# A block of two mixers and routed experts on one core: low parts of projection pieces on VectorE, scores of two heads by turns in two banks, norms for 128 tokens

## The chip, the core and the metric

The kernel runs on one core of a Trainium2 chip. A core has TensorE (matmuls and weight loads, results in PSUM), VectorE, ScalarE, GpSimd, and SyncE, whose queue (SP) issues most transfers to 16 DMA engines. The metric is the device time of one execution in microseconds, median of several runs.

## What is computed

One layer over 2048 tokens of width 1024: a modulated norm, one projection `w_in` of 5792 columns, two recurrent mixers on parts of it, two output projections that are gated and summed, then a router and 32 experts of which each token takes two. The part that matters here is the second recurrence's set-up (RWKV-7, 8 heads of 64):

```
p = p + mu * (prev - p)
r, k, v, wd, ad, gd = split(p)
kk = heads(k * k_k)
kk = kk * rsqrt(maximum(sum(kk * kk, axis=-1), 1e-24))
# per token: state = state * w + (state @ -kk) (kk * a)^T + v k^T ;  y = state @ r
```

and the projection itself, `proj = h @ w_in`, in fp32 accuracy.

## The kernel before

**Projections.** `w_in` is applied in four rounds (g = 0..3) of 512 tokens and 46 tiles of 128 columns (`win_tiles`). fp32 accuracy comes from splitting both sides into a high part (rounded to fp32r) and a low part (the rest): each tile is 8 x 3 matmuls of 128x512 (lines 778 to 780). A tile's weights are two pieces of 512 x 128 (`parts`). In round 0 a piece is loaded raw (two raw buffers, line 759), ScalarE makes its high part (760), GpSimd its low part (761), and SP stores both for the later rounds (763), which load them ready-made (756). Pieces have four buffers. The evicted tile goes to DRAM (line 794). `mixed` does the same for the two output projections, with 16 pieces split once.

**Mixers.** The 2048 tokens go through both mixers in 16 blocks of 128. For the RWKV mixer, `rw_prep` sets a block up: norms of `kk` per head (matmuls with `hind`, line 196), then scores of each chunk of 64 tokens: for each half `hp` of the partitions (heads are stacked two to a tile, 64 rows each) four matmuls into the one bank `rp` (224) and four VectorE instructions that scale and mask them into `Gc` (226). From `Gc` a 32x32 triangular system is cut out through DRAM (`Nd`, `Nl`), solved by a recurrence of 62 VectorE instructions (243, 244) and brought back (`Pd`, `Pa`). `rw_chain` (matmuls `mm` of line 296, `px<-R,Pa` among them) runs the state over the chunks, and `hg_block` is the other mixer (HGRN2), whose transposes and outputs use the bank `ht` and whose score levels use `hl`. The five banks `rp`, `xy`, `px`, `ht`, `hl` and three of the projections fill PSUM.

**Order.** Instructions are recorded in the code's order, which lays projection tiles between the mixers' pieces (`fill`), and are then put in order per engine by the framework's scheduler. Each engine and SP's queue run in that order and wait where a semaphore is not yet there. From the experts on the order is the program's own.

Of the kernel before, what the change touches and what calls it, by code (L numbers as in the profile page):

```python
# [6 lines left out]
FP = mybir.dt.float32  # L7
# [3 lines left out]
AF = mybir.ActivationFunctionType  # L11
OP = mybir.AluOpType
# [5 lines left out]
TB = 128  # L18
# [130 lines left out]
def rw_prep(k, b):  # L149

    nc = k.nc
    NC = TB // 64
    g, off = divmod(b * TB, 512)
    wk, w2p, ps = k.wk, k.wk2, k.ps
# [15 lines left out]
    for i, (bias, dst) in enumerate(((k.w0, sw), (k.a0, a))):  # L170
        pt = ps.tile(f4, FP, name="rp")
# [14 lines left out]
    kkr = wk.tile(f4, FP, name="t3")  # L186
    nc.gpsimd.tensor_tensor(kkr, k_, k.kkc[:, :, None].to_broadcast(f4), OP.mult)
    AR = w2p.tile([128, 4, NC, 128], FP, name="AR", bufs=2); BK = wk.tile([128, 4, NC, 128], FP, name="BK")
    c4 = lambda t: t.rearrange("p m (c t) -> p m c t", t=64)
    sq = BK[:, :, :, 64:128]; nc.scalar.activation(sq, c4(kkr), AF.Square)  # L190

    pt = ps.tile(f4, FP, name="rp")
    nrm = pt[0:64, 0, 0:8 * NC].rearrange("p (c h) -> p c h", c=NC)
    for c in range(NC):
        for m in range(4):
            nc.tensor.matmul(nrm[:, c, 2 * m:2 * m + 2], sq[:, m, c], k.hind, start=(c + m == 0), stop=True,
                             skip_group_check=True)
    iv = k.iv[b % 2]
    nc.vector.tensor_scalar(iv[0:64], nrm, 1e-24, 2.0, op0=OP.max, op1=OP.mult)
    nc.vector.reciprocal(iv[0:64], iv[0:64])  # L200
    nc.gpsimd.tensor_tensor(AR[:, :, :, 64:128], c4(r_), c4(Gm), OP.mult)
    ARf = AR.rearrange("p m c x -> p (m c) x")
# [14 lines left out]
    Gs = []  # L217
    for c in range(NC):
        Gc = w2p.tile([128, 2, 4, 128], FP, name="Gc", bufs=4)
        for hp in range(2):  # L220
            pt = ps.tile([128, 4, 128], FP, name="rp")
            h = slice(hp * 64, hp * 64 + 64)
            for m in range(4):
                nc.tensor.matmul(pt[:, m], BK[h, m, c, :], AR[h, m, c, :], start=(m == 0), stop=True, skip_group_check=True)  # L224
            for m in range(4):
                nc.vector.scalar_tensor_tensor(Gc[:, hp, m], pt[:, m], iv[:, c, 2 * m + hp:2 * m + hp + 1], k.gmask, op0=OP.mult, op1=OP.mult)  # L226
        for hf in range(2):
            q = slice(hf * 32, hf * 32 + 32)
            nc.sync.dma_start(Nd[hf, c * 8:(c + 1) * 8].rearrange("x s t -> s x t"), Gc[q, :, :, q].rearrange("p a m t -> p (a m) t"))
        Gs.append(Gc)  # L230
# [24 lines left out]
    for c in range(NC):  # L255
        pt = ps.tile([128, 512], FP, name="rp")
        for m in range(4):
            nc.tensor.transpose(pt[:, m * 128:(m + 1) * 128], BK[:, m, c, :], k.ident)
        t = w2p.tile([128, 4, 128], FP, name="BT", bufs=4)
# [5 lines left out]
    for c2 in range(NC // 2):  # L265
        pt = ps.tile([128, 512], FP, name="rp")
# [10 lines left out]
    pt = ps.tile(f4, FP, name="rp")  # L277
# [473 lines left out]
def parts(k, key, src):  # L751

    nc = k.nc
    w = k.ld.tile([128, 2, 4, 128], FR, name="w", bufs=4)
    if key in k.split:
        nc.sync.dma_start(w.bitcast(FP), k.split[key])
        return w
    raw = k.ld.tile([128, 4, 128], FP, name="wraw", bufs=2)
    nc.sync.dma_start(raw, src.rearrange("(k p) n -> p k n", p=128))
    nc.scalar.copy(w[:, 0], raw)  # L760
    nc.gpsimd.tensor_tensor(w[:, 1], raw, w[:, 0].bitcast(FP), OP.subtract)  # L761
    k.split[key] = k.dr1.tile([128, 2, 4, 128], FP, name="W" + key)
    nc.sync.dma_start(k.split[key], w.bitcast(FP))
    return w


def win_tiles(k, I, hT, g, tiles):

    nc = k.nc
    dst_of = {"rw": k.RWP, "hg": k.HGP, "gt": k.GTP}  # L770
    hi, lo = hT
    for group, ti, c0 in tiles:
        dst = dst_of[group]
        W = [parts(k, f"{group}{ti}_{q}", I['w_in'][0, q * 512:(q + 1) * 512, c0:c0 + 128]) for q in range(2)]
        pt = k.pm.tile([128, 512], FP, name="mm", bufs=3)
        for kk in range(8):
            whi, wlo = (W[kk // 4][:, j, kk % 4] for j in range(2))
            nc.tensor.matmul(pt, whi, hi[kk // 2][:, kk % 2], start=(kk == 0), stop=False)  # L778
            nc.tensor.matmul(pt, whi, lo[kk // 2][:, kk % 2], start=False, stop=False)  # L779
            nc.tensor.matmul(pt, wlo, hi[kk // 2][:, kk % 2], start=False, stop=(kk == 7))  # L780
        ev = k.ld.tile([128, 512], FP, name="ev", bufs=3)
        if group == "rw":
            nc.scalar.activation(ev, pt, AF.Identity, scale=k.omu[:, ti:ti + 1])  # L783
            mu = k.mu[:, ti:ti + 1]; ca = k.carry[:, ti:ti + 1]
            nc.vector.scalar_tensor_tensor(ev[:, 1:512], pt[:, 0:511], mu, ev[:, 1:512], op0=OP.mult, op1=OP.add)  # L785
            nc.vector.scalar_tensor_tensor(ev[:, 0:1], ca, mu, ev[:, 0:1], op0=OP.mult, op1=OP.add)
            nc.vector.tensor_copy(ca, pt[:, 511:512])
        else:
            k.flip ^= 1
            if k.flip:  # L790
                nc.scalar.copy(ev, pt)
            else:
                nc.vector.tensor_copy(ev, pt)
        nc.sync.dma_start(dst[g][ti], ev)
# [620 lines left out]
def build(ctx, tc, I, out, NE=32):  # L1415
# [22 lines left out]
    with ExitStack() as c2:  # L1438
# [15 lines left out]
        for g in range(5):  # L1454
# [14 lines left out]
            for i in range(4 if g < 4 else 2):  # L1469
                b = g * 4 - 2 + i  # L1470
                ws = WS[i] if g < 4 else MS[i]
                if g == 4 and i == 1:
                    list_init(k)
                    router_consts(k, I)
                with hp(tc, b + 1 >= HP[0]):
                    nxt = rw_prep(k, b + 1) if -1 <= b < 15 else None
                fill(ws[0])
                if b >= 0:
                    with hp(tc, b >= HP[1]):
                        rw_chain(k, b, prep)  # L1480
                fill(ws[1])
                if b >= 0:
                    with hp(tc, b >= HP[2]):
                        hg_block(k, b)
                fill(ws[2])
                prep = nxt
# [37 lines left out]
```

## Time and profile before

| | |
|---|---|
| median of 3 runs | 2983.82 us (2966.77 to 2990.27) |
| profiled execution | 2984.66 us, span 2982.8 us |
| TensorE matmuls busy | 2766.5 us (93%) |
| weight loads | 2257.7 us (76%) |
| VectorE, ScalarE, GpSimd | 1985.8 us (67%), 1286.4 us (43%), 943.0 us (32%) |
| mean granted TensorE clock | 0.965 |

Busy times are sums over the whole span and say little about one stage: the span holds a start of some 45 us, the four rounds with the mixers (to about 1830 us), the output projection and the router (to about 2210 us) and the experts. In the rows below PE is TensorE's matmuls, PEld its weight loads, DVE VectorE, ACT ScalarE, POOL GpSimd, SPq SyncE's queue; PEclk is the granted clock as a share of full speed. A matmul's duration overlaps the next one's start, so prices are read from starts. An fp32 matmul stands as two passes, a projection matmul as one.

### The profile page before, as it was taken

How to read it: one execution, taken by the hardware profiler on the slowest of the kernel's cores; microseconds unless marked ns; L12 is line 12 of the kernel's file. 1: busy time of each engine (PE TensorE's matmuls, PEld its weight loads, DVE VectorE, ACT ScalarE, POOL GpSimd, SP SyncE). 2: the span in 40 equal slices, each digit the busy share in tenths (PEclk: the TensorE clock that was granted, in tenths of full speed). 3: DMA queues.
4: the chain of work that ended last, by engine and by line, in shares of the span. 5: the costliest groups of instructions: out<-in, count | busy, mean ns of one | idle time of the engine just before them, and what ended most of it. 6: DMA issues, size and time to landing. Idle time of an engine off the chain costs nothing. (4 is left out here: it accounts for less than half of the span.)

```text
span 2982.8 us, 45842 instructions
## 1 busy us (share of the span) xinstructions
PE 2766.5 (93%) x15562; PEld 2257.7 (76%) x15562; DVE 1985.8 (67%) x4010; ACT 1286.4 (43%) x2188; POOL 943.0 (32%) x1092
## 2 busy tenths in 40 slices
PE   6989999999999999999999999899959999999992
PEld 4667788887888888888888777788857777777771
DVE  6164666683677666677547876446565798989983
ACT  4332544432343523333233544322224566767772
POOL 3344643322332313342233453332441121112112
PEclk9989999999999999999999989999979999999996
DMA  8897786687565776566555678886448799999996
GB/s 257 285 322 239 224 256 196 196 252 219 174 211 176 232 246 191 180 223 202 187 183 173 187 231 289 302 294 212 142 158 256 264 363 347 363 347 359 373 314 229
DMA packets 460698, 734.65 MB, mean 246 GB/s; under 512 B 115569, under 2 KB 277361, under 8 KB 460354
## 3 DMA queue, kind: packets, MB, share of 16 engines
q1 hardware_dynamic: 448114, 696.68, 69.8%
q0 software_dynamic: 11088, 29.60, 4.3%
q10 hardware_dynamic: 1152, 4.19, 0.4%
q8 instruction: 165, 2.70, 0.4%
q14 instruction: 179, 1.47, 0.1%
HBM read 561.81 MB, written 175.39 MB: 247 GB/s over the span
## 5 line engine op out<-in xcount | busy, mean ns | idle before, releaser
L778 PE MATMUL mm<-hThi,w 128*128 128x512 f32 x1472 | 596.4, 406 | 19.1 <-ACT hThi L667 10.1
L780 PE MATMUL mm<-hThi,w 128*128 128x512 f32 x1472 | 595.4, 405 | 9.2 <-POOL w L761 8.6
L779 PE MATMUL mm<-hTlo,w 128*128 128x512 f32 x1472 | 592.1, 402 | 1.0 <-DVE hTlo L668 0.9
L1206 DVE TENSOR_TENSOR wlo<-raw,whi 128x1024 fp32r<-128x1024 f32 x404 | 484.1, 1254 | 46.1 <-ACT whi L1205 21.5
L1205 ACT CAST whi<-raw 128x1024 fp32r<-128x1024 f32 x408 | 405.7, 1057 | 206.0 <-PE U L931 48.6
L778 PEld LDWEIGHTS mm<-hThi,w 128*128 128x128 f32 x1472 | 282.3, 192 | 88.2 <-ACT hThi L667 10.2
L780 PEld LDWEIGHTS mm<-hThi,w 128*128 128x128 f32 x1472 | 282.0, 192 | 79.5 <-POOL w L761 20.2
L779 PEld LDWEIGHTS mm<-hTlo,w 128*128 128x128 f32 x1472 | 282.1, 192 | 61.2 <-DVE hTlo L668 3.6
L1294 POOL DMA_INDIRECT X<-y,lists x33 | 72.3, 2190 | 497.4 <-DVE y L1292 449.6
L243 DVE TENSOR_TENSOR pr<-Pl,Nl 128x2 f32<-128x2 f32 (+30 forms) x496 | 202.5, 408 | 12.0
L451 POOL TENSOR_TENSOR Xq<-h,kf 128x256 f32<-128x256 f32 x96 | 80.2, 835 | 399.0 <-PE hl L470 116.9
L761 POOL TENSOR_TENSOR w<-wraw,w 128x512 fp32r<-128x512 f32 x108 | 145.2, 1346 | 171.0 <-ACT w L760 153.4
L760 ACT CAST w<-wraw 128x512 fp32r<-128x512 f32 x108 | 66.8, 619 | 152.1 <-DMA wraw<-in_w_in_dram 114.0
L244 DVE TENSOR_REDUCE Pl<-pr 128x1 f32<-128x2 f32 (+30 forms) x496 | 124.0, 250 | 12.0
L856 PE MATMUL mm<-hThi,w 128*128 128x512 f32 x256 | 104.9, 412 | 11.7 <-ACT hThi L667 6.8
L296 PE MATMUL xy<-UV,Gc 128*64 128x64 f32 (+1 forms) x1536 | 114.0, 223 | 0.6 <-ACT UV L305 0.6
L1236 PE MATMUL G<-whi,xh 128*128 128x512 f32 x256 | 104.9, 410 | 9.5 <-PEq L1367 8.3
L296 PEld LDWEIGHTS xy<-UV,Gc 128*64 128x64 f32 (+1 forms) x1536 | 95.6, 127 | 19.4 <-issue 7.1
L857 PE MATMUL mm<-hTlo,w 128*128 128x512 f32 x256 | 105.3, 411 | 2.4 <-DVE hTlo L668 2.4
L785 DVE SCALAR_TENSOR_TENSOR ev<-mm,mu,ev 128x511 f32<-128x511 f32 x56 | 41.8, 747 | 97.1 <-ACT ev L783 93.5
L226 DVE SCALAR_TENSOR_TENSOR Gc<-rp,iv,gmask 128x128 f32<-128x128 f32 x256 | 71.9, 343 | 51.7 <-PE rp L224 51.4
L858 PE MATMUL mm<-hThi,w 128*128 128x512 f32 x256 | 103.8, 406 | 0.0
(492 smaller groups left out, 5924.3 us busy)
## 6 DMA issues: line engine op xcount, KB each, us to landing
raw<-in_exp_w_gate_dram SPq DMA_DIRECT2D x126, 512.0 KB
raw<-in_exp_w_up_dram SPq DMA_DIRECT2D x126, 512.0 KB
raw<-in_exp_w_down_dram SPq DMA_DIRECT2D x124, 512.0 KB
w<-Whg SPq DMA_DIRECT2D x96, 512.0 KB
w<-Wgt SPq DMA_DIRECT2D x96, 512.0 KB
w<-Wrw SPq DMA_DIRECT2D x84, 512.0 KB
wraw<-in_w_in_dram SPq DMA_DIRECT2D x92, 256.0 KB
Whg<-w SPq DMA_DIRECT2D x32, 512.0 KB
```

Source lines behind the costliest of these rows:

```text
L243: nc.vector.tensor_tensor(pv, Pl[:, :ni, :ns], Nl[:, :ns, t_][:, None, :].to_broadcast([128, ni, ns]), OP.mult)
L244: nc.vector.tensor_reduce(Pl[:, :ni, t_], pv, AX.X, OP.add)
L296: mm = lambda *a_, **kw: nc.tensor.matmul(*a_, skip_group_check=True, **kw)
L761: nc.gpsimd.tensor_tensor(w[:, 1], raw, w[:, 0].bitcast(FP), OP.subtract)
L778: nc.tensor.matmul(pt, whi, hi[kk // 2][:, kk % 2], start=(kk == 0), stop=False)
L779: nc.tensor.matmul(pt, whi, lo[kk // 2][:, kk % 2], start=False, stop=False)
L780: nc.tensor.matmul(pt, wlo, hi[kk // 2][:, kk % 2], start=False, stop=(kk == 7))
L856: nc.tensor.matmul(pt, w[:, 0, kk], hi[o // 2][:, o % 2], start=(kk == 0), stop=False)
L857: nc.tensor.matmul(pt, w[:, 0, kk], lo[o // 2][:, o % 2], start=False, stop=False)
L1205: s.nc.scalar.copy(hi, raw)
L1206: eng.tensor_tensor(lo, raw, hi.bitcast(FP), OP.subtract)
L1236: mm = lambda *a, **kw: nc.tensor.matmul(*a, skip_group_check=True, **kw)
```

## The change

1. `parts`: the low part of a piece (line 761) is computed by VectorE and not by GpSimd.
2. `rw_prep`, norms: four matmuls for 128 tokens (line 195 after) take the place of eight for 64 tokens (line 196 before); two VectorE instructions bring them to the 64 rows of `iv`. The squares lie in the first half of `BK`'s bytes instead of every second 64 columns.
3. `rw_prep`, scores: the eight matmuls of a chunk are written head by head in turn, one on partitions 0 to 63 into `rp`, one on 64 to 127 into `ht` (line 223 after); the evictions follow.

```diff
-    sq = BK[:, :, :, 64:128]; nc.scalar.activation(sq, c4(kkr), AF.Square)
+    sq = BK.rearrange("p m c x -> p (m c x)")[:, 0:4 * TB].rearrange("p (m t) -> p m t", t=TB); nc.scalar.activation(sq, kkr, AF.Square)
     pt = ps.tile(f4, FP, name="rp")
-    nrm = pt[0:64, 0, 0:8 * NC].rearrange("p (c h) -> p c h", c=NC)
+    nrm = pt[:, 0, 0:8]
+    for m in range(4):
+        nc.tensor.matmul(nrm[:, 2 * m:2 * m + 2], sq[:, m], k.hind, start=(m == 0), stop=True, skip_group_check=True)
+    iv = k.iv[b % 2]
     for c in range(NC):
-        for m in range(4):
-            nc.tensor.matmul(nrm[:, c, 2 * m:2 * m + 2], sq[:, m, c], k.hind, start=(c + m == 0), stop=True,
-                             skip_group_check=True)
-    iv = k.iv[b % 2]
-    nc.vector.tensor_scalar(iv[0:64], nrm, 1e-24, 2.0, op0=OP.max, op1=OP.mult)
+        nc.vector.tensor_scalar(iv[0:64, c], nrm[c * 64:c * 64 + 64], 1e-24, 2.0, op0=OP.max, op1=OP.mult)
...
-        for hp in range(2):
-            pt = ps.tile([128, 4, 128], FP, name="rp")
-            h = slice(hp * 64, hp * 64 + 64)
-            for m in range(4):
+
+        pts = [ps.tile([128, 4, 128], FP, name=n) for n in ("rp", "ht")]
+        for m in range(4):
+            for h, pt in zip((slice(0, 64), slice(64, 128)), pts):
                 nc.tensor.matmul(pt[:, m], BK[h, m, c, :], AR[h, m, c, :], start=(m == 0), stop=True, skip_group_check=True)
+        for hp, pt in enumerate(pts):
             for m in range(4):
                 nc.vector.scalar_tensor_tensor(Gc[:, hp, m], pt[:, m], iv[:, c, 2 * m + hp:2 * m + hp + 1], k.gmask, op0=OP.mult, op1=OP.mult)
...
-    nc.gpsimd.tensor_tensor(w[:, 1], raw, w[:, 0].bitcast(FP), OP.subtract)
+    nc.vector.tensor_tensor(w[:, 1], raw, w[:, 0].bitcast(FP), OP.subtract)
```

What the scheduler makes of it is seen in the order of the instructions. On VectorE, in round 0 during the first block's set-up (`acc` belongs to the modulation's sums, `ev` to evicted tiles), before:

```order
L213 TENSOR_TENSOR BK<-t_1177,t_1210 128x8x64
L657 TENSOR_SCALAR ev<-mm,A_424,mod_422 128x128
L635 TENSOR_TENSOR xss_1594<-xss_1594 128x1
L86 TENSOR_SCALAR rst_x<-xss_1594 128x1
L226 SCALAR_TENSOR_TENSOR Gc<-rp,iv_510,gmask 128x128 x4
L607 TENSOR_SCALAR acc<-xin,cs 128x512
```

and in the changed kernel:

```order
L761 TENSOR_TENSOR w<-wraw,w 128x512
L793 COPY ev<-mm 128x512
L226 SCALAR_TENSOR_TENSOR Gc<-rp,iv_510,gmask 128x128 x4
L226 SCALAR_TENSOR_TENSOR Gc<-ht,iv_510,gmask 128x128 x4
L657 TENSOR_SCALAR ev<-mm,A_424,mod_422 128x128 x2
L761 TENSOR_TENSOR w<-wraw,w 128x512
L609 SCALAR_TENSOR_TENSOR acc<-xin,cs,acc 128x512
```

The low parts of pieces now stand in VectorE's queue among evictions that wait for TensorE, and both halves of a chunk's scores are evicted one after the other.

On TensorE, in round 1, a chunk's scores before (`px` and `xy` are the RWKV chain's):

```order
L779 MATMUL mm<-hTlo_8108,w 128x512
L224 MATMUL rp<-AR,BK 128x128 x4
L296 MATMUL px<-UV,BT 128x128 x4
L296 MATMUL xy<-UV,Gc 64x64 x8
L780 MATMUL mm<-hThi_8102,w 128x512
...
L780 MATMUL mm<-hThi_8103,w 128x512
L224 MATMUL rp<-AR,BK 128x128 x4
L778 MATMUL mm<-hThi_8103,w 128x512
```

and a chunk's scores of a block in the changed kernel's round 1, where the turns go on to eight rows:

```order
L779 MATMUL mm<-hTlo_8087,w 128x512
L296 MATMUL px<-UV,BT 128x128 x2
L223 MATMUL rp<-AR,BK 128x128
L223 MATMUL ht<-AR,BK 128x128
L223 MATMUL rp<-AR,BK 128x128
L223 MATMUL ht<-AR,BK 128x128
...
L223 MATMUL ht<-AR,BK 128x128
L296 MATMUL px<-UV,BT 128x128 x2
```

Two runs of four with projection matmuls between them became one run of eight that changes halves at each matmul.

On TensorE in another block of that round of the changed kernel (`ht<-Shg,Xq` and `ht<-vT,scT` are the other mixer's outputs, `ht<-ident,o` its last transposes):

```order
L503 MATMUL ht<-Shg,Xq 128x128 x4
L505 MATMUL ht<-vT,scT 128x128 x4
L508 MATMUL hl<-vT,kT 128x128 x4
L223 MATMUL rp<-AR,BK 128x128 x4
L296 MATMUL px<-R,Pa 32x64 x8
...
L520 MATMUL ht<-ident,o_11119 128x128 x4
L296 MATMUL px<-UV,BT 128x128 x2
...
L778 MATMUL mm<-hThi_8082,w 128x512
L779 MATMUL mm<-hTlo_8086,w 128x512
L223 MATMUL ht<-AR,BK 128x128 x4
```

Here the half that goes to `rp` stands together and the half that goes to `ht` stands some 45 rows later, behind the other mixer's use of that bank.

## Rows read from the trace of the kernel before

**Rows 1.** Stretches: busy us (instructions) of each engine, PEclk, DMA share, GB/s.
```profile
core 0: us, PE busy (x) PEld busy (x) DVE busy (x) ACT busy (x) POOL busy (x), PEclk, DMA share, GB/s
...
60.00:160.00 100.00, 88.91 (x361) 64.23 (x359) 21.01 (x57) 31.54 (x58) 38.50 (x34) 0.99 0.88 280
160.00:260.00 100.00, 88.52 (x410) 67.06 (x409) 67.69 (x158) 35.14 (x82) 47.21 (x47) 0.87 0.88 283
260.00:400.00 140.00, 135.19 (x801) 108.21 (x801) 72.55 (x168) 58.89 (x110) 76.60 (x80) 0.96 0.78 241
400.00:1750.00 1350.00, 1329.87 (x8582) 1105.90 (x8581) 899.93 (x2206) 509.67 (x1025) 443.09 (x600) 0.99 0.66 205
```

**Rows 2.** Timeline, a score run: start us, us, engine line op out<-in xcount.
```profile
601.71 0.39 PE L778 MATMUL mm<-hThi,w 128*128 128x512 f32 x1
602.02 1.16 PE L224 MATMUL rp<-AR,BK 64*128 64x128 f32 x8
...
603.69 0.40 PE L778 MATMUL mm<-hThi,w 128*128 128x512 f32 x1
...
604.39 0.39 PE L778 MATMUL mm<-hThi,w 128*128 128x512 f32 x1
...
602.02 0.96 PEld L224 LDWEIGHTS rp<-AR,BK 64*128 64x128 f32 x8 [0.36 <-DVE h L425]
```

**Rows 3.** Timeline of TensorE, a run of eight passes on all 128 rows.
```profile
650.54 0.40 PE L780 MATMUL mm<-hThi,w 128*128 128x512 f32 x1
650.78 1.00 PE L479 MATMUL hl<-Xq 128*128 128x64 f32 x8
...
652.13 0.39 PE L780 MATMUL mm<-hThi,w 128*128 128x512 f32 x1
```

**Rows 4.** Timeline of TensorE, a run of the norms.
```profile
1616.42 0.40 PE L779 MATMUL mm<-hTlo,w 128*128 128x512 f32 x1
1616.95 1.09 PE L196 MATMUL rp<-hind,BK 128*64 128x2 f32 x16
...
1618.54 0.40 PE L779 MATMUL mm<-hTlo,w 128*128 128x512 f32 x1
```

**Rows 5.** Timeline of SP, ScalarE and GpSimd, one piece's way in round 0.
```profile
88.81 0.43 SPq L759 DMA_DIRECT2D wraw<-in_w_in_dram  x1
...
92.47 0.62 ACT L760 CAST w<-wraw 128x512 fp32r<-128x512 f32 x1 [0.70 <-DMA wraw<-in_w_in_dram]
...
93.17 1.29 POOL L761 TENSOR_TENSOR w<-wraw,w 128x512 fp32r<-128x512 f32 x1 [2.57 <-ACT w L760]
94.48 0.32 SPq L763 DMA_DIRECT2D Wrw<-w  x1
...
94.85 0.43 SPq L759 DMA_DIRECT2D wraw<-in_w_in_dram  x1
```

**Rows 6.** A stretch, instructions of line 778 alone: PE busy (x), PEld busy (x).
```profile
60.00:160.00 100.00, 46.37 (x116) 21.78 (x116) 0.99 0.88 280
```

**Rows 7.** A stretch of three tiles at a steady pace, columns as in rows 1.
```profile
97.00:115.00 18.00, 17.35 (x73) 12.86 (x72) 3.10 (x9) 5.79 (x9) 6.79 (x7) 1.00 0.94 301
```

**Rows 8.** Lines 761 and 668: count, ns min/median/max, first and last start us.
```profile
L761 POOL TENSOR_TENSOR w<-wraw,w x108: 1257/1287/2610, 42.0 to 1769.0; 128x512 fp32r<-128x512 f32 x108
...
L668 DVE TENSOR_TENSOR hTlo<-rwin,hThi x3: 715/1030/1136, 46.0 to 48.1; 128x512 fp32r<-128x512 f32 x3
```

**Rows 9.** Timeline of VectorE beside GpSimd, and line 213's durations.
```profile
174.11 1.29 POOL L761 TENSOR_TENSOR w<-wraw,w 128x512 fp32r<-128x512 f32 x1
174.18 1.76 DVE L213 TENSOR_TENSOR BK<-t,t 128x512 f32<-128x512 f32 x1 [1.37 <-POOL t L212]
...
L213 DVE TENSOR_TENSOR BK<-t,t x16: 665/809/3319, 174.2 to 1726.2; 128x512 f32<-128x512 f32 x16
```

**Rows 10.** Timeline, a block's last score evictions and the first matmul on `Pa`.
```profile
1568.31 1.13 DVE L226 SCALAR_TENSOR_TENSOR Gc<-rp,iv,gmask 128x128 f32<-128x128 f32 x4 [4.63 <-PE rp L224]
...
1623.19 0.52 PE L296 MATMUL px<-R,Pa 32*32 32x64 f32 x6
```

**Rows 11.** VectorE's waits from 160 to 420 us: total us, times, longest us.
```profile
DVE BT L260 <- PE rp L258: 13.7, 4, 8.6
DVE Gc L226 <- PE rp L224: 13.6, 5, 6.8
DVE scT L480 <- PE hl L479: 11.0, 4, 4.8
DVE ev L793 <- ACT w L760: 8.9, 1, 8.9
```

## Prediction

> **What bounds the kernel now.** I read the stretches first, then the TensorE timeline inside them, then the queues. Between 400 and 1750 us, 45% of the span, TensorE is busy for 1329.9 of 1350 us at a granted clock of 0.99, while VectorE, ScalarE and GpSimd stand at 67%, 38% and 33% [rows 1]. There the time is the sum of what TensorE has to do, and only less TensorE work (or a new hole in it) moves the end. Before 400 us it is less full: 88.9 us of 100 between 60 and 160, 88.5 of 100 at a clock of 0.87 between 160 and 260, 135.2 of 140 after that [rows 1]. From 1800 us on nothing is touched except the last two blocks of the mixers. The part from the experts on stands in the same order in both programs.
>
> What TensorE does with the touched matmuls is seen when a run of them stands alone between projection matmuls. Three projection matmuls take 0.70 us (603.69 to 604.39) [rows 2]. A run of 8 score passes (4 matmuls of fp32, two passes each, 64 rows by 128 columns) makes 1.98 us of what would be 0.70, so it costs 1.28 [rows 2]. A run of 8 passes that uses all 128 rows costs 1.59 - 0.70 = 0.89 us, 0.112 a pass [rows 3]. The passes themselves are alike, so entering and leaving the half array costs 1.28 - 0.89 = 0.39 us a run. The norms' run (16 passes, 128 rows by 64 columns, 0.06 us each) costs 2.12 - 0.70 = 1.42 us, of which 16 x 0.06 = 0.96 is passes and 0.46 is entering and leaving [rows 4].
>
> In the first round (60 to 160 us) something else is the limit: a loop. A piece's load is issued at 88.81, its cast starts at 92.47 when it has landed, GpSimd's low part runs from 93.17 to 94.46, SP stores the piece at 94.48 and issues the load that reuses the raw buffer at 94.85 [rows 5]. That is 6.04 us for one of two raw buffers, so one tile (two pieces) in 6.04 us, where TensorE needs 24 x 0.233 = 5.6. Over the whole stretch 116 matmuls of line 778, eight to a tile, make 14.5 tiles in 100 us, 6.9 us each [rows 6].
>
> **The low parts (line 761): 108 pieces, 92 of them in the first round.** GpSimd takes 1.29 us at the median; VectorE's nearest row, the same subtraction on 128x512, took 0.715 at its shortest and about 1.03 beside a busy GpSimd [rows 8]. I take 0.7, so the loop loses 0.6 and becomes 5.44, under TensorE's 5.6. SP's order helps too: both loads of a tile now stand ahead of the store of an evicted tile. But the DMA engines were 94% busy in a stretch at that pace of 6.04 [rows 7], which puts their own floor at about 5.7 us. Bounds: 0 if the transfers only take longer, 14.5 x (6.9 - 5.6) = 19 us if TensorE is always fed. Nearest to the rows is the loop's 0.6 cut by the DMA floor: 14.5 x 0.5 = **-7 us**. From 160 to 400 us the tiles are slowed by the mixers, not by this loop: 0. The 16 pieces of the output projections, near 1750 us: 0.
>
> VectorE gets 108 x 0.7 = 76 us more. It is busy 21% to 68% of these stretches [rows 1]; its idle time is the cover, and it is thin where VectorE waits for others with pieces queued behind (the slower rival). Something comes back: its subtraction of line 213 took 1.76 us beside GpSimd's line 761 against 0.665 at its shortest [rows 9], so each piece taken from GpSimd also takes such a block away. Both stay at 0 in the sum, since VectorE is not the bound.
>
> **Norms.** Eight matmuls a block on 64 columns become four on 128: 16 passes of 0.06 (0.96 us) become 8 of 0.112 (0.90), and they no longer leave the full array. The one more VectorE instruction a block (on 64x8 values) lies in VectorE's idle third. The squares now lie partly where line 207 writes BK, so that write has to wait for four matmuls; VectorE reads the norms just ahead of it anyway, so the order asks nothing new.
>
> **Scores.** In TensorE's order the 256 score matmuls stood in 83 runs and stand in 51 (one bank made the scheduler put them apart). Over all lines the number of places where one matmul's array shape (rows by columns of its weights) differs from the next falls from 664 to 573. At half of 0.39 each, the 91 give 17.7 us. I count **-15 us**, because some lie before 400 us where TensorE also waits. Bounds: 0 (a change of shape costs nothing where TensorE waits anyway) and 91 x 0.23 = 21 (half of the norms' 0.46).
>
> The turns themselves are fewer than the diff suggests. The scheduler keeps seven of the sixteen blocks by turns; in nine it sets four heads on one half, and the other four later, when the second mixer has given back its bank. Only 78 times does a matmul follow one on the other half of the array. In the rows no such pair stands, so the price is open: 0 if the passes still follow each other at 0.112 us, 78 x 0.112 = 8.7 us if each hides one pass. In one half, loads are already covered: 8 loads span 0.96 us beside 8 matmuls in 1.16 [rows 2], so what is left to overlap is load and stream of one half beside those of the other. I take the middle, **-5 us**.
>
> The Trainium skill, page TensorE: Matmul & The Clock Gate (The mechanism), says that a weight load overlaps matmuls in flight only where the row group differs. The trace differs: in one row group eight loads and eight matmuls share the same microsecond. By the rule the 78 turns would each take a load of 0.12 us (0.96 by 8) out of the line, 9 us; by the row there is nothing there to take. The Trainium skill, page TensorEngine Tiling (Array Packing) (Key Properties), says that different tiles load and multiply in parallel; no run here shows it, and by it the turns give the 8.7 us, as in the first rival.
>
> **The shared bank.** Where the halves are set apart, a block's last scores come later in TensorE's order than its first ones by some forty rows and more. From them hang the eviction, two DMAs out and in, the recurrence of 62 instructions and two DMAs again. In one block that way took from 1568.31 to 1623.19, 55 us [rows 10]. The new order leaves one or two blocks with less TensorE work than that in between. **+2 us**; bounds 0 and 15 (three blocks by 5).
>
> **Sum.** -7 - 15 - 5 + 2 = -25 us. The profiled execution took 2984.66 us (span 2982.8), within 1 us of the median 2983.82. 2984.7 - 25 gives **2960 us**.
>
> **Rivals.**
> *It gains more.* The turns hide a pass each and the loop falls to TensorE's floor: -19 - 18 - 9 = -46, 2939 us. For: every piece of it has its bound in the rows. Against: the DMA share of 0.94 [rows 7].
>
> *Nothing comes of it.* DMA holds the loop, passes follow each other as now, and the late halves leave holes that eat most of what the shapes save: -12 + 8 = -4, 2980 us. For: the way of 55 us in rows 10 is two thirds of a block's time. Against: the cost of a shape is plain in two kinds of run [rows 2, 4].
>
> *Slower: VectorE's queue holds the pieces.* Between 160 and 420 us VectorE waits with its queue stopped: 13.7 us for line 258's transposes, 13.6 for the scores, 11.0 for the second mixer, up to 8.9 in one wait [rows 11]. GpSimd's queue did not hold pieces behind such waits for TensorE. Now pieces stand behind them, and SP's stores and the next loads behind those. Four piece buffers are two tiles, 11 us of cover when full; it decides from the point where a wait comes with that cover empty, as the loop of rows 5 leaves it. If all three sums reach TensorE, +38 us, plus some 10 for the halved clock after holes (0.87 there already): 2984.7 + 48 - 20 (shapes and turns) = 3013 us. Against: the order sets most pieces between short instructions of the recurrence.
>
> **How the numbers follow.** The forecast (2945 to 2972) has 0.60, more gain 0.12, nothing 0.18, slower 0.10. The range 2932 to 2992 leaves out the slower rival and the ends, about 2 in 10. About 1% (30 us) is what a measurement of this kernel can tell from no change. 1% under the median is 2954: the gaining rival and half of 0.45 within the forecast lie under it, 0.12 + 0.27 = 0.39. Over 3013.7 lies most of the slower rival, 0.09. The rest is 0.52.
>
> **What would show it.** Right: line 778's count in 60 to 160 us rises from 116 to about 125, and SP's cycle in a steady tile is under 5.8 us; score runs of 16 passes by turns cost under 16 x 0.112 + 0.39 = 2.18 us; TensorE stays over 98% between 400 and 1750. Wrong: TensorE's waits for VectorE's w at line 780 in the first 400 us grow past today's; or waits of px or ht of several microseconds appear after the split blocks.

## The result and the profile after

The changed kernel took 2960.88 us at the median of 10 runs (2947.89 to 2968.14), the kernel before 2980.38 in the 10 runs beside it. The ratio is 0.9938, with a 95% interval of 0.9924 to 0.9952, so 18 us less (interval: 14 to 23). The forecast was 2960. The profiled execution has a span of 2955.1 us, 27.7 less than before.

The stretches of the changed kernel, with the columns of [rows 1]:

```profile
60.00:160.00 100.00, 94.52 (x381) 69.41 (x379) 41.21 (x97) 35.58 (x71) 4.27 (x9) 0.97 0.95 304
160.00:260.00 100.00, 89.22 (x433) 70.77 (x434) 68.14 (x166) 35.37 (x77) 15.54 (x22) 0.95 0.97 316
260.00:400.00 140.00, 134.39 (x875) 111.65 (x874) 96.23 (x227) 63.92 (x121) 42.07 (x59) 0.95 0.77 238
400.00:1750.00 1350.00, 1319.68 (x8552) 1101.74 (x8551) 904.11 (x2300) 503.88 (x1028) 417.25 (x581) 0.98 0.67 206
```

TensorE is fuller from 60 to 160 us (94.5 instead of 88.9) and has a better clock from 160 to 260 (0.95 instead of 0.87). From 400 to 1750 it is *less* busy than before, 1319.7 instead of 1329.9, and the DMA share of the first stretches is up from 0.88 to 0.95 and 0.97. Line 778 in the first of these stretches, which answers [rows 6], and the page's groups of TensorE's third product and of the low parts (busy, mean ns | idle before, what ended it):

```profile
60.00:160.00 100.00, 48.95 (x121) 23.13 (x121) 0.97 0.95 304
```

```profile
L780 PE MATMUL mm<-hThi,w 128*128 128x512 f32 x1472 | 590.1, 401 | 0.2 <-DVE w L761 0.2
...
L761 DVE TENSOR_TENSOR w<-wraw,w 128x512 fp32r<-128x512 f32 x108 | 79.2, 733 | 105.5 <-ACT w L760 102.9
```

121 matmuls stand where 116 stood, and TensorE waits 0.2 us in all for a low part. VectorE needs 733 ns for one, close to the 0.7 that I took. Its longest wait from 160 to 420 us answers [rows 11], and line 212 (line 213 before) answers [rows 9]:

```profile
DVE w L761 <- ACT w L760: 46.5, 28, 5.6
```

```profile
L212 DVE TENSOR_TENSOR BK<-t,t x16: 617/684/1764, 167.3 to 1693.6; 128x512 f32<-128x512 f32 x16
```

The 13.7, 13.6 and 11.0 us that VectorE used to wait there for TensorE are not among its waits of 1.3 us and more there; what it waits for now is the next piece's cast on ScalarE. Line 212 is at 684 ns at the median instead of 809.

Now the touched matmuls. A run of 16 score passes by turns, and a run of the norms, in the timeline of TensorE (start us, us, engine line op out<-in xcount); the first is to be read with [rows 2], the second with [rows 4]:

```profile
177.99 0.39 PE L779 MATMUL mm<-hTlo,w 128*128 128x512 f32 x1
178.31 0.60 PE L223 MATMUL rp<-AR,BK 64*128 64x128 f32 x3
178.64 0.37 PE L223 MATMUL ht<-AR,BK 64*128 64x128 f32 x1
178.75 0.27 PE L223 MATMUL rp<-AR,BK 64*128 64x128 f32 x1
178.85 0.27 PE L223 MATMUL ht<-AR,BK 64*128 64x128 f32 x1
178.86 0.27 PE L223 MATMUL rp<-AR,BK 64*128 64x128 f32 x1
178.96 0.27 PE L223 MATMUL ht<-AR,BK 64*128 64x128 f32 x1
178.97 0.27 PE L223 MATMUL rp<-AR,BK 64*128 64x128 f32 x1
...
179.72 0.50 PE L780 MATMUL mm<-hThi,w 128*128 128x512 f32 x1
```

```profile
437.15 0.40 PE L779 MATMUL mm<-hTlo,w 128*128 128x512 f32 x1
437.39 0.95 PE L195 MATMUL rp<-hind,BK 128*128 128x2 f32 x8
...
438.74 0.39 PE L779 MATMUL mm<-hTlo,w 128*128 128x512 f32 x1
```

The passes of the two halves start in pairs, 0.01 us apart (178.85 and 178.86, 178.96 and 178.97), a pair every 0.11 us. From the first pass to the next projection matmul the 16 passes take 1.41 us (178.31 to 179.72), although three passes of one half stand in front of the turns and some of the other behind them. Where all 16 take turns, it is 1.09 us:

```profile
1413.18 0.37 PE L223 MATMUL rp<-AR,BK 64*128 64x128 f32 x1
1413.19 0.37 PE L223 MATMUL ht<-AR,BK 64*128 64x128 f32 x1
...
1414.27 0.50 PE L779 MATMUL mm<-hTlo,w 128*128 128x512 f32 x1
```

The norms cost 1.59 - 0.70 = 0.89 us a block instead of 1.42.

### The profile page after: what moved, and what is told of

Read it like the earlier page. It is cut to its first block, busy times and chain, and to the rows that moved or that the text cites. A ratio compares the mean times of both kernels' runs of the same rounds, so it can differ in the third digit from the quotient of the medians.

```text
span 2955.1 us, 45546 instructions
## 1 busy us (share of the span) xinstructions
PE 2736.4 (93%) x15434; PEld 2243.8 (76%) x15434; DVE 2014.1 (68%) x4134; ACT 1275.2 (43%) x2183; POOL 798.4 (27%) x984
## 5 line engine op out<-in xcount | busy, mean ns | idle before, releaser
L243 DVE TENSOR_TENSOR pr<-Pl,Nl 128x2 f32<-128x2 f32 (+30 forms) x496 | 186.0, 375 | 11.7
L761 DVE TENSOR_TENSOR w<-wraw,w 128x512 fp32r<-128x512 f32 x108 | 79.2, 733 | 105.5 <-ACT w L760 102.9
L244 DVE TENSOR_REDUCE Pl<-pr 128x1 f32<-128x2 f32 (+30 forms) x496 | 124.3, 251 | 12.6
L1236 PE MATMUL G<-whi,xl 128*128 128x512 f32 x256 | 101.6, 397 | 0.0
L1236 PE MATMUL G<-wlo,xh 128*128 128x512 f32 x256 | 101.5, 397 | 0.0
```

What stands on the lines that cost most here:

```text
L243: nc.vector.tensor_tensor(pv, Pl[:, :ni, :ns], Nl[:, :ns, t_][:, None, :].to_broadcast([128, ni, ns]), OP.mult)
L244: nc.vector.tensor_reduce(Pl[:, :ni, t_], pv, AX.X, OP.add)
L1236: mm = lambda *a, **kw: nc.tensor.matmul(*a, skip_group_check=True, **kw)
```

## How the programs are compared

Summed from start to start, without TensorE's waits, over the trace up to the last matmul of the output projections, the scores take 55.9 us of TensorE instead of 73.4 and the norms 13.8 instead of 17.8. That is 21.5 us less, and the time fell by 18. It looks as if the one explained the other. The runs show that it does not.

For all programs below I divide the span at two places: the first projection matmul of tile 46, where round 0 ends, and the first matmul of the experts (line 1236). Two rows of stretches give it, the columns as above; before (46.0, 447.3, 2239.2):

```profile
46.00:447.30 401.30, 370.84 (x1913) 285.52 (x1913) 213.16 (x493) 157.08 (x304) 192.22 (x195) 0.95 0.83 263
447.30:2239.20 1791.90, 1726.82 (x10708) 1439.59 (x10706) 1151.57 (x2767) 641.50 (x1213) 605.69 (x797) 0.97 0.66 210
```

and after:

```profile
45.70:421.80 376.10, 352.94 (x1881) 278.94 (x1881) 234.46 (x560) 152.93 (x299) 73.03 (x103) 0.96 0.89 281
421.80:2213.70 1791.90, 1714.52 (x10613) 1431.80 (x10611) 1157.30 (x2822) 634.54 (x1213) 582.07 (x783) 0.97 0.66 210
```

Round 0 is 25.2 us shorter. In these two executions the rest is as long as before, 1791.9 us, although TensorE works 12.3 us less in it: its idle time (length less busy time) is 77.4 us instead of 65.1. In the table "idle" is that idle time of the second part, "half clock" the time there with a granted clock of 0.5 (1.2 GHz instead of 2.4), and "work" is length - idle - half of the half-clock time, a rough measure of what TensorE had to do. The low parts of e16_late are on GpSimd for the first 16 tiles and on VectorE from there. Ratios are of medians, each to the runs of before beside it.

| program | low parts on | round 0 | then to experts | idle | half clock | work | ratio to before (95%) |
|---|---|---|---|---|---|---|---|
| before | GpSimd | 401.3 | 1791.9 | 65.1 | 97.6 | 1678.0 | 1 |
| e14_flip_before | GpSimd | 398.4 | 1809.3 | 75.9 | 118.9 | 1674.0 | 1.0062 (1.0040 to 1.0085) |
| e3_norms | GpSimd | 401.0 | 1807.0 | 75.5 | 116.8 | 1673.1 | 1.0072 (1.0059 to 1.0085) |
| e2_scores | GpSimd | 397.3 | 1809.4 | 82.7 | 118.5 | 1667.4 | 1.0065 (1.0052 to 1.0078) |
| e13_scores_norms | GpSimd | 404.2 | 1805.3 | 82.6 | 122.5 | 1661.4 | 1.0090 (1.0069 to 1.0110) |
| e16_late | both | 383.9 | 1782.2 | 64.4 | 80.6 | 1677.5 | 0.9952 (0.9935 to 0.9969) |
| e1_low | VectorE | 376.1 | 1800.4 | 68.6 | 101.1 | 1681.2 | 0.9945 (0.9926 to 0.9964) |
| e9_low_norms | VectorE | 381.9 | 1782.3 | 63.5 | 80.8 | 1678.4 | 0.9948 (0.9935 to 0.9961) |
| after | VectorE | 376.1 | 1791.9 | 77.4 | 95.8 | 1666.6 | 0.9938 (0.9924 to 0.9952) |
| e4_same_half | VectorE | 377.9 | 1793.3 | 73.3 | 90.8 | 1674.6 | 0.9941 (0.9917 to 0.9964) |
| e5_four_four | VectorE | 376.4 | 1796.4 | 79.2 | 99.0 | 1667.6 | 0.9907 (0.9888 to 0.9926) |
| e15_flip_after | VectorE | 376.7 | 1806.3 | 82.5 | 120.2 | 1663.7 | 0.9950 (0.9927 to 0.9973) |
| e11_twice | VectorE | 387.9 | 1838.8 | 82.4 | 130.4 | 1691.1 | 1.0152 (1.0137 to 1.0166) |
| e8_mm_bank | VectorE | 442.6 | 1894.6 | 143.4 | 287.0 | 1607.7 | 1.0488 (1.0469 to 1.0506) |

The stretches are those of one profiled execution each, the ratio is of many runs. How far one execution can be trusted is seen where nothing differs: from the first matmul of the experts to the end all programs have the same matmuls, and this part took 735.5 to 750.4 us in the 14 traces, with 60 to 81 us of it at the half clock, most in the longest and least in the shortest. The runs of the kernel before alone lie between 2967 and 2990 us. So a difference of some 10 us in one stretch counts here only where several programs agree on it.

## The experiments

### The low parts alone

```diff
-    nc.gpsimd.tensor_tensor(w[:, 1], raw, w[:, 0].bitcast(FP), OP.subtract)
+    nc.vector.tensor_tensor(w[:, 1], raw, w[:, 0].bitcast(FP), OP.subtract)
```

> The kernel before with the low parts on VectorE alone; 79 score runs and 649 changes of shape, against 83 and 664. Theory A: -7 us from the loop in the first 160 us, about -3 us from the 15 fewer changes of shape, ratio 0.9965; line 778 stands about 125 times between 60 and 160 us instead of 116. Rival C (the loop is worth more because it also frees the rest of round 0): -15 us or more, ratio 0.995 or less, with the lead over before still growing between 160 and 400 us. Rival D (VectorE's queue holds pieces): ratio above 1.

2964.96 us, 0.9945. One line of the change gives nearly all of its gain (16 of 18 us), as rival C had it, and round 0 is as short as after, 376.1.

### The low parts from the seventeenth tile on

```diff
-    nc.gpsimd.tensor_tensor(w[:, 1], raw, ...)
+    (nc.gpsimd if len(k.split) < 32 else nc.vector).tensor_tensor(w[:, 1], raw, ...)
```

> The kernel before, with the low parts of the first 32 pieces (16 tiles, to about 159 us) on GpSimd as before and those of the other 76 on VectorE. The step of the forecast (the loop of one raw buffer is loosened in the first 160 us, nothing comes from 160 to 400 us): no gain, 2977 to 2984 us, with tile 16 and tile 32 as late as before (159 and 309 us). The reading of the trace with all low parts moved (tile 16 was 8 us earlier, tile 32 24 us, and what the stretch from 160 to 310 us gave came from waits and from the clock that fell after them): tile 16 at 159 us, tile 32 some 14 us earlier, and the time 2965 to 2972 us.

2962.90 us, 0.9952. The stretch of line 778 and TensorE's waits from 60 to 450 us (line waited for: us in total, times, longest us):

```profile
60.00:160.00 100.00, 47.11 (x119) 22.18 (x118) 1.00 0.89 284
```

```profile
PE mm L780 <- POOL w L761: 6.2, 13, 0.6
PE mm L778 <- ACT w L760: 5.0, 5, 1.8
```

The loop of the first 160 us is back, with TensorE waiting 13 times for GpSimd's w, and tile 16 starts at 156.9 us instead of 152.5 after (159.2 before). The gain is there all the same: tile 32 starts 13.8 us earlier than before, round 0 is 17.4 us shorter, 14.9 of them behind the start of tile 16, and the time can't be told from that of all low parts moved. So most of the gain sits behind the first 160 us, where the first blocks of the mixers run, and not in the loop of the raw buffers.

### The scores alone, the norms alone, both together

The scores' and the norms' parts of the diff, put into the kernel before one by one and together; GpSimd keeps the low parts.

> The kernel before with the scores' part of the change alone (two banks, heads by turns); low parts stay on GpSimd, norms as before. The scheduler makes 59 score runs instead of 83 and 68 turns from one half to the other; 636 changes of array shape instead of 664. Theory A (every microsecond that TensorE saves ahead of the experts reaches the end): TensorE's time for the scores falls from 73.4 us to about 58 and the time falls with it, 2981 - 15 = 2966 us. Theory B (what TensorE saves inside the mixers comes back as waits elsewhere, and the gain of the whole change is that of the low parts): the scores' time falls as well, but the time stays within 2975 to 2985 us.

2998.18 us, 1.0065: 19 us slower.

> The kernel before with the norms' part alone (four matmuls for 128 tokens instead of eight for 64). The order has 76 score runs and 638 changes of array shape instead of 83 and 664. Theory A: TensorE's time for the norms falls from 17.8 us to 13.8 and 13 changes of shape of 0.2 us go besides, so 2981 - 6 = 2975 us. Theory B: 2978 to 2984 us, no difference that can be told.

2999.03 us, 1.0072: 21 us slower.

> The kernel before with the scores' and the norms' part together; low parts stay on GpSimd (54 score runs, 598 changes of shape). Alone, each of the two made the kernel some 20 us slower, though TensorE needed 14 us less for the scores and 3 to 4 us less for the norms. Theory C (each part has a cost of its own, a wait that it brings): the two add up, 2980 + 40 = 3020 us. Theory D (any other order of the kernel before costs about 20 us, because the order of before happens to wait little): 2985 to 3002 us, no sum. Theory A of the first experiments (TensorE's saving counts): 2960 us.

3004.92 us, 1.0090: 27 us slower, not 40, so theory C does not hold, and theory D's 3002 is just passed. Neither theory of the first two runs foresaw a loss. Yet the scores do take less TensorE time (59.8 us instead of 73.4 in e2_scores), and the norms too (14.7 instead of 17.8 in e3_norms). The second part of e2_scores:

```profile
443.50:2252.90 1809.40, 1726.66 (x10683) 1437.89 (x10682) 1155.37 (x2797) 634.77 (x1205) 604.63 (x798) 0.97 0.65 208
```

Work falls by 10.6 us against before (1678.0 to 1667.4), idle time grows by 17.6 and time at the half clock by 21.

### Low parts and norms, without the scores

> The kernel before with the low parts on VectorE and the norms for 128 tokens, scores as before (73 runs, 617 changes of shape). Set beside the low parts alone (2965 us) and the whole change (2961 us). Theory A: 2965 - 6 = 2959 us, and then the scores' turns of the whole change would be worth nothing or less. Theory B: 2965 us as with the low parts alone, within 3 us.

2961.17 us, 0.9948: as with the low parts alone and as the whole change. So with the low parts on VectorE the norms cost nothing and bring nothing that shows. And against this program the scores' part of the change takes 11.8 us of work off the second part (1678.4 to 1666.6) and adds 13.9 of idle time and 15 at the half clock. TensorE's waits from the end of round 0 to the experts (as above) in e9_low_norms, where lines after the norms have one number less:

```profile
PE px L295 <- DMA Pa<-Pd: 4.7, 3, 2.4
```

and in the changed kernel:

```profile
PE px L296 <- DMA Pa<-Pd: 5.3, 4, 2.5
PE rp L173 <- DVE S L169: 3.4, 1, 3.4
...
PE hl L479 <- DVE pr L243: 2.7, 1, 2.7
```

About 29 us of the idle time lie in the routing behind the output projections, in every program alike. The holes that differ are small, of many kinds, and belong to the mixers' own chains: up to the last matmul of the RWKV chain TensorE is idle for 22.8 us in e9_low_norms and for 35.8 after. No single wait took the gain.

### Both heads from one half

```diff
-                nc.tensor.matmul(pt[:, m], BK[h, m, c, :], AR[h, m, c, :], ...
+                nc.tensor.matmul(pt[:, m], BK[0:64, m, c, :], AR[0:64, m, c, :], ...
```

> The changed kernel with one edit: both heads of a turn are read from partitions 0 to 63 (the odd heads' scores are then wrong; nothing else is left out). The order of the instructions, 51 score runs, 573 changes of array shape and 78 turns between the two banks stay as they are; what is gone is that the two matmuls of a turn lie on different halves of the array. Theory A (halves of the array work side by side, one pass of 0.112 us hidden per turn): a run of 16 score passes between projection matmuls goes from 1.41-1.51 us back to 16 x 0.112 + 0.39 = 2.18, and the kernel is 6 to 10 us slower than the changed one (78 x 0.112 = 8.7), ratio to before about 0.997. Rival B (it was the two banks, or the order): runs of 16 passes stay at 1.4 to 1.5 us and the ratio stays near 0.994.

2962.83 us, 0.9941. The order of all instructions is that of the changed kernel, so only the overlap of the halves is gone. The same run as above, in the timeline of TensorE:

```profile
178.64 0.39 PE L779 MATMUL mm<-hTlo,w 128*128 128x512 f32 x1
178.96 0.93 PE L223 MATMUL rp<-AR,BK 64*128 64x128 f32 x6
179.73 0.83 PE L223 MATMUL ht<-AR,BK 64*128 64x128 f32 x6
180.40 0.38 PE L223 MATMUL rp<-AR,BK 64*128 64x128 f32 x2
180.63 0.38 PE L223 MATMUL ht<-AR,BK 64*128 64x128 f32 x2
180.94 0.50 PE L780 MATMUL mm<-hThi,w 128*128 128x512 f32 x1
```

The 16 passes take 1.98 us (178.96 to 180.94) instead of 1.41. Reckoned as in the prediction, with 0.70 us for three projection matmuls taken off, this run costs 2.17 us against 1.60 after, and the one at 1413 us 2.28 against 1.39. The scores' TensorE time goes from 55.9 to 68.1 us, so the halves do work side by side, and 78 turns are worth 12.2 us of TensorE. The time is worth less: the ratios differ by 0.0003 with an uncertainty of 0.0028, that is +1 us, 9 at most. So theory A held for the run and not for the time. In the second part work grows by 8.0 us, and idle time falls by 4.1 and time at the half clock by 5.

### Four heads on one half, then four on the other

```diff
-        for m in range(4):
-            for h, pt in zip((slice(0, 64), slice(64, 128)), pts):
+        for h, pt in zip((slice(0, 64), slice(64, 128)), pts):
+            for m in range(4):
```

> The changed kernel with the eight score matmuls of a chunk written four on the lower half, then four on the upper half, into the same two banks: 50 runs and 572 changes of shape, but 17 turns instead of 78. Theory A: 61 x 0.112 = 6.8 us slower than the changed kernel, ratio to before about 0.996; the gain that stays is that of the fewer shapes and of the low parts. Rival B (two banks alone do it): same as the changed kernel within 2 us. Order luck between the two could be some 5 us either way.

2952.48 us, 0.9907 (0.9888 to 0.9926), with 17 turns instead of 78 and 61.6 us for the scores instead of 55.9. It is the shortest of all programs, 0.0031 under the changed kernel with an uncertainty of 0.0024. Neither theory had that. It beats both kernels, but I can't say that it does so because of its order of heads: a trade that changes no work at all moved the time more (below), and in the traces its round 0 and second part together are 4.8 us longer than after's; what is shorter is the part from the experts on (735.5 against 741.4), where the two programs do not differ.

### The second half's scores in a bank of the projections

```diff
-        pts = [ps.tile([128, 4, 128], FP, name=n) for n in ("rp", "ht")]
+        pts = [ps.tile([128, 4, 128], FP, name="rp"), k.pm.tile([128, 4, 128], FP, name="mm", bufs=3)]
```

> The changed kernel with the second half's scores in one of the projections' three banks instead of the second mixer's: 37 score runs instead of 51, 102 turns instead of 78, 498 changes of shape instead of 573. Theory A (shapes and turns are prices that TensorE pays): 75 x 0.195 = 14.6 and 24 x 0.112 = 2.7 us less, 17 us faster than the changed kernel, ratio to before about 0.988. Rival E (a projection bank held by four evictions on VectorE leaves TensorE waiting between tiles): TensorE's waits for banks of mm grow and the gain is eaten, ratio 0.993 or more.

3125.96 us, 1.0488, far slower; 66 us of the loss against the changed kernel are in round 0 already. It has the fewest runs (37), the most turns (102) and the fewest changes of shape (498) of the programs then at hand. TensorE from 400 to 1750 us, and its longest waits for the mixers after round 0:

```profile
400.00:1750.00 1350.00, 1273.01 (x7845) 1068.36 (x7844) 830.91 (x2059) 459.14 (x935) 374.42 (x532) 0.93 0.60 189
```

```profile
PE px L296 <- ACT R L302: 15.4, 10, 2.7
...
PE xy L296 <- ACT UV L305: 11.0, 7, 3.2
...
PE px L296 <- ACT R L308: 6.3, 8, 1.2
```

The steps of the recurrence now stand bare: TensorE waits 32.7 us for R and UV in these 25 waits, where in the changed kernel each of the three is at 1.5 us or less. With a projection bank lent to the scores there are not enough projection matmuls between the steps to cover them; that the bank is what is missing is argued and was not tested apart. Idle time is 143.4 us instead of 77.4, and time at the half clock 287.0 us instead of 95.8. The wait that rival E named is not the one: line 778 waits 2.8 us in the whole span for evictions of the projections (line 793). Fewer runs and shapes were worth nothing against that.

### Every score matmul twice

```diff
-        for m in range(4):
+        for m in (0, 1, 2, 3, 0, 1, 2, 3):
```

> The changed kernel with every score matmul of the first mixer issued twice into the same place (the second time starts the bank anew, so the values are the same). TensorE gets 256 matmuls more, 512 passes. By the runs of 16 passes by turns, which cost 1.41 to 1.51 us with 0.39 of it for entering and leaving the half array, a pass is 0.066 us, so some 34 us of TensorE time are added where it is over 97% busy. Theory A: they reach the end nearly whole, 2961 + 30 = 2991 us or more. Theory B (other engines and queues set the pace of the mixers, TensorE has slack that the projections fill): less than a third of it, 2961 to 2972 us.

3018.13 us, 1.0152, some 60 us more than after. The scores take 102.7 us instead of 55.9, 46.8 more (I had expected 34: a good part of the added passes do not find a partner). So TensorE work that is *added* arrives at the end in full, and holes with it (idle time 82.4 us instead of 77.4, half clock 130.4 instead of 95.8); its order is another one too (58 score runs, 595 changes of shape).

### The same work in another order

The evicted tiles that go to ScalarE and VectorE by turns (those of the second mixer's columns and of the gates) trade places. Nothing is added or removed, but the scheduler lays another order.

```diff
-            if k.flip:
+            if not k.flip:
                 nc.scalar.copy(ev, pt)
```

In the kernel before:

> The kernel before with one word more: the evicted tiles of the gates that went to VectorE go to ScalarE and the other way round. No work is added or taken away on any engine but one eviction in two trades places; yet the scheduler makes another order (73 score runs instead of 83, 652 changes of shape instead of 664). Theory D (the order alone moves the time by some 20 us): 2990 to 3005 us, or at the least 6 us away from the kernel before on either side. Theory C (time belongs to the parts, the order averages out): 2975 to 2986 us.

2997.52 us, 1.0062: 18 us slower for no more work. Its second part, and TensorE's waits in it:

```profile
444.80:2254.10 1809.30, 1733.42 (x10676) 1446.06 (x10674) 1145.00 (x2762) 636.69 (x1205) 600.89 (x796) 0.97 0.64 209
```

```profile
PE px L296 <- DMA Pa<-Pd: 7.0, 3, 3.1
PE rp L196 <- ACT BK L190: 6.0, 4, 1.8
```

Neither of these two waits stands among those of 0.4 us and more that the kernel before has in this part. Its idle time there is 65.1 us, the flipped one's 75.9. The loss lies in the second part; round 0 is as before (398.4).

In the changed kernel:

> The changed kernel with the same trade of evictions between ScalarE and VectorE. No work is added or taken away, and the order becomes another one (60 score runs instead of 51, 65 turns instead of 78, 582 changes of shape instead of 573). Theory D: at least 6 us away from the changed kernel's 2961 us, 2967 to 2985 us if its order is a good one. Theory C: 2956 to 2966 us.

2966.58 us, 0.9950 (0.9927 to 0.9973). The difference to the changed kernel, 0.0012 with an uncertainty of 0.0027, can't be told from none, so the theory that any order costs 6 us or more is not borne out here. Its profiled execution has a second part of 1806.3 us, 14 longer than that of after.

## Why the prediction was right, and where it was not

The time came out within 1 us of the forecast, but not by the sum as it was put: that it is so near is luck. One term was too small by some 9 us and another too large by some 20; the gain is 18 to 20 us instead of 25, and that 2960 is met all the same is because the kernel before stands at 2980 us in the runs beside it, 4 less than the execution from which I started.

**The low parts: -7, measured -16 alone, with -23 in round 0 on the mean.** The step for the first 160 us held: tile 16 starts 6.7 us earlier. (The term was put too high for its own rows: a loop of 6.04 us cut to the DMA floor of 5.7 gives 0.34 a tile, 5 us, and not 0.5.) What failed is the sentence that the mixers set the pace from 160 to 400 us and that nothing comes there. From tile 16 to the end of round 0:

```profile
159.20:447.30 288.10, 270.75 (x1517) 213.97 (x1517) 181.93 (x426) 117.84 (x237) 143.69 (x151) 0.93 0.82 259
152.50:421.80 269.30, 252.81 (x1487) 206.34 (x1486) 187.26 (x463) 114.66 (x232) 63.05 (x89) 0.95 0.87 276
```

The first row is of before, the second of after. This is not one order's luck: leaving out e8_mm_bank and e11_twice, round 0 takes 376 to 382 us in all six programs with all low parts on VectorE, against 397 to 404 in the five with GpSimd, and the stretch behind tile 16 takes 269 to 276 against 285 to 293. e16_late has 273 there without the first 16 tiles. The total of 16 us alone would not show it, since a trade of evictions moved the time by 18.

Where the 23 us lie can be read from the means of those eleven traces. TensorE's idle time in round 0 falls from 33 to 23 us, half of that up to tile 16, where its waits for a low part (6.8 of the 8.6 us that before has from 60 to 450 us) are gone, and half behind it, in small waits of many kinds. Time at the half clock falls from 38 to 32 us, worth 3, which is no more than traces differ. The rest, some 9 us, is less work: about 40 passes fewer of the mixers and others stand in round 0 (at 0.11 us each an estimate of 4 us, most of which only moves to the second part), and the shortened scores and norms stand in more of the six programs than of the five. Behind tile 16 GpSimd is busy for less than half as long (63 us instead of 144), and line 212's VectorE instructions are shorter. I noted VectorE's slowing beside GpSimd [rows 9] and set it to nothing because VectorE wasn't the bound. Whether this slowing or GpSimd's freed queue is what eased the mixers' waits was not taken apart.

**Shapes and turns: -20, measured -21.5 in TensorE's time (4.0 of it the norms') and about 0 in the kernel's.** The sum of the work was good by two errors that cancel. Without the turns the scores fall by 5.3 us (73.4 to 68.1 in e4_same_half) and the norms by 4.0, so the fewer shapes gave at most 9.3 instead of 15; and the turns alone exceed my bound: 12.2 us, or 0.156 a turn, where I had allowed 78 x 0.112 = 8.7. I had let a turn hide one pass; a matmul has two, and both may run beside those of the other half. That eight loads fit beside eight matmuls [rows 2] did not say what paces a pass: in these runs it seems to be the load (last section), and turns let two loads run at once. What failed is the first premise, that between 400 and 1750 us only the sum of TensorE's work moves the end. In three pairs of programs that differ by the scores' part alone (before and e2_scores, e3_norms and e13_scores_norms, e9_low_norms and after) work in the second part falls by 10.6, 11.7 and 11.8 us, and idle time grows by 17.6, 7.1 and 13.9, half-clock time by 21, 6 and 15. Up to the last matmul of the RWKV chain the idle time grows by 15.2, 12.6 and 13.0, at least as much as the work falls; the half-clock times differ by no more than those of the experts' part do between traces. By the ratios the scores' part costs 19 us in the first pair, and in the others 5 us (uncertain by 7) and -3 (uncertain by 6): in none does it gain what TensorE saves. The share of over 98% that I named as a mark of being right was missed (1319.7 of 1350 is 97.8%). TensorE is the fullest engine there, so more work costs time (e11_twice), but it also waits in short holes for the mixers' chains, and these grew as the matmuls got shorter. That it only comes to the same waits earlier is my reading; the rows show that the holes grow, not why each does.

**Late halves, +2.** The waits of px for Pa that I named do appear (5.3 us after, none of 0.4 us or more in the second part before), but e9_low_norms, without the shared bank, has 4.7, and e14_flip_before, without any of the change, 7.0. So they are not peculiar to the shared bank.

**Norms, 0.** Right in time with the low parts on VectorE (e9_low_norms). On TensorE they gave 4.0 us.

**The rivals.** VectorE's queue did not hold the pieces: line 780 waits 0.2 us for them, less than before. (That rival's own 3013 us also lies under the 3013.7 above which I put most of its chance.) "Nothing comes of it" had the right mechanism for the scores (holes eat what they save), and was wrong on the low parts. "More gain" had the turns right on TensorE and still failed, for the same holes.

**The other marks.** Line 778 rose from 116 to 121 and not to 125. SP's cycle in a steady tile stayed at 5.6 to 6.1 us (line 759's loads of one buffer at 98.71, 104.83 and 110.82 us, of the other at 101.76 and 107.37), at a DMA share of 0.95 over the stretch, as the weighing against [rows 7] had it. The two runs of 16 passes by turns between projection matmuls cost 1.39 and 1.60 us, under the 2.18.

**What stays open.** Of the five orders with GpSimd's low parts that of before is the only good one: the four others, one of them with no change of work, are 18 to 27 us slower. Against those four, VectorE's low parts are worth 39 us (mean ratios 1.0072 and 0.9940, the latter over after, e1_low, e4_same_half, e5_four_four, e9_low_norms, e15_flip_after and e16_late). Against before they are worth 18. Round 0 explains 22 of the 39. Why the second part, too, is shorter on the mean with VectorE (1793 us over those seven, 1808 over the four), although only the 16 pieces of the output projections are split there, is not settled, and 4 us more are in the experts' part, which no program changes; the spread among orders, 1782 to 1809, is larger than that. Nor do the runs say whether the order of before is luck or whether something in the kernel was fitted to it.

## What to carry to other kernels

TensorE busy for 98% of a stretch is not proof that less TensorE work is less time: look in the same stretch for the short waits on chains, which may take back what shorter matmuls save. Where a scheduler lays the order, run one variant that changes no work before believing a difference of half a per cent; here such a variant cost 18 us, as much as the whole change gained. And an engine that is idle enough on the average can still be in the way: taking 1.3 us a piece off GpSimd made the first round 23 us shorter on the mean of eleven traces.

## What the runs showed of the hardware

Matmuls on rows 0 to 63 and on rows 64 to 127 run side by side, passes starting 0.01 us apart: 16 of them take 1.09 us where all take turns and 1.41 where some do not, instead of 1.98 where both read the same half. Their weight loads start side by side as well:

```profile
178.85 0.19 PEld L223 LDWEIGHTS ht<-AR,BK 64*128 64x128 f32 x1
178.86 0.19 PEld L223 LDWEIGHTS rp<-AR,BK 64*128 64x128 f32 x1
```

The Trainium skill, page TensorEngine Tiling (Array Packing) (Key Properties), says that different tiles load and multiply in parallel; these runs agree. The gain ends there, on TensorE: it did not reach the kernel's time.

What a pass of these fp32 matmuls costs goes with the columns of its weights and not with the columns that stream past them. With 128 columns of weights it is about 0.11 us, whether 2 columns stream (the norms after, 8 passes in 0.81 us), 64 [rows 3] or 128 (e4_same_half, two passes each 0.22 us); with 64 columns of weights it is 0.06 [rows 4]. So the weights seem to set the pace of a pass, and turns help because two halves take theirs at once; no run was made to test that.

The granted clock was at a half for 98 us of the second part before, for 96 after and for 287 in e8_mm_bank, where idle time was 65, 77 and 143 us. In round 0 it was at a half for 41 us before and 31 after. The program with by far the most idle time, e8_mm_bank, also has by far the most time at the half clock; but between before and after idle time grew by 12 us and half-clock time did not. In the experts' part, with the same matmuls in every program, half-clock time alone differed by 22 us between traces and the time by 15.
